# Modulation products of four channel blocks in four column groups, from the ninth block on

## The chip, the cores and the metric

The kernel runs on one core of one Trainium2 chip. The metric is the device time of one execution in microseconds (us). The kernel before takes 954.64 us, the median of three runs (954.42 to 954.87).

## The reference

One layer of a hybrid state-space and convolution block. `x` is 512 x 2048 and the context is 256 x 2048. What matters here is the first step:

```
def _adaln(cond, w_ada, b_ada):
    mod = jax.nn.silu(cond) @ w_ada + b_ada          # w_ada is 2048 x 6144
    return mod[..., :D_MODEL], mod[..., D_MODEL:2 * D_MODEL], mod[..., 2 * D_MODEL:]
def _modulate(v, shift, scale):
    return (_layernorm(v) * (1.0 + scale) + shift).astype(v.dtype)
...
    shift, scale, gate = _adaln(c, w_ada, b_ada)
    shift_c, scale_c, gate_c = _adaln(c_ctx, w_ada, b_ada)
    h = _modulate(x, shift[:, None], scale[:, None])
    hc = _modulate(ctx, shift_c, scale_c)
    u, z_s5, v, bg, cg, z_cv = _split_proj(h @ w_in)
    ...
        u_c = hc @ w_in[:, :D_S5]
```

Every one of the 2048 channels needs a shift and a scale for the latent rows and a shift and a scale for the context rows: a product of two vectors of 2048 with 2048 x 4096 weights, 32 MB in all. The rest of the layer (the state-space scan, the convolution, the gates, the output projection and the last LayerNorm) is not touched.

## The kernel before

**Blocks and tiles.** The channels stand in 16 blocks of 128. Block k's shift and scale weights arrive as two tiles of 1 MB, (k, 0) and (k, 1), one for each half of the 2048 inputs. They share a ring of seven buffers, `wa` (`RB = 7`), with the six 1 MB tiles of `x` and the context. `fill()` asks for the next tile in the order of the list `ring` as soon as the tile seven places earlier has been marked used; the request goes out on GpSimd's queue (POOL), and the instruction waits there until the matmuls that read the old contents of the buffer are done.

**Products.** `ada(k, hf)` runs eight matmuls for one tile: the stationary operand is a 128 x 32 slice of `cs` (the two condition vectors after SiLU, padded to 32 columns), the moving operand 256 columns of the tile. Matmul j writes partitions 32 * (j mod 4) on of the PSUM tile `aps`, so four matmuls in a row go to four column groups of TensorE, and four partial sums of block k stand below each other. `combine(k)` then copies `aps` to SBUF on ScalarE (`part`), transposes it in two TensorE instructions into `cps` (the other half of the same PSUM bank), and adds the four partial sums and the bias on VectorE into `ss`, 0.5 us in three instructions.

**The loop of the head.** `head()` holds all of this and the first quarter of the input projection. Its steady part is the loop over k from 3 to 15. One step does, in this order: `ada(k, 0)`, `ada(k, 1)`, the copy of `combine(k)`, a first `half()`, the transposition and sums of `combine(k)`, a second `half()`, and `mod(k)`. The two `half()` calls run the projection for block k - 2: nine 128 x 512 matmuls for the latent rows and twelve 128 x 256 ones for the context in the first, twelve more 128 x 256 ones in the second (`lat`, `cxt`, PSUM tiles `acc`). The third matmul of each group reads `wlo`, the low part of the projection weights, which VectorE splits off two items ahead. `mod(k)` makes the modulated channels: ScalarE writes `hi`, VectorE `xl`, `xc` and `lo`, for use two steps later. `some(us)` lets VectorE do a planned number of microseconds of the state-space parameters (`s5_params`) before and after the main part of `mod`. After k = 15 two more steps of `half()` finish the projection of blocks 14 and 15.

**Order.** The order of the instructions on every engine is the order in which this code is written; each engine works its own queue strictly in that order. A clock of planned costs (`_Clock`) decides where the background generators are called later in the kernel. `s5_params` waits for `room`, since it takes two `wa` buffers itself, and copies its powers (`PW`) on POOL, in the same queue as the `wa` requests.

Of the kernel before, what the change touches and what calls it, by code (L numbers as in the profile page):

```python
# [12 lines left out]
OP = mybir.AluOpType  # L13

P = 128
D = 2048
KT = 16
# [127 lines left out]
def tile_hybrid_s5_shortconv(  # L145
# [8 lines left out]
    ve, ac = _Timed(nc.vector, "dve", clk), _Timed(nc.scalar, "act", clk)  # L154
    pe, gp, sp = _Timed(nc.tensor, "pe", clk), _Timed(nc.gpsimd, "pool", clk), _Timed(nc.sync, "sp", clk)
# [30 lines left out]
    cs = base.tile([P, KT, 32], F32, name="cs")  # L186
    ss = base.tile([P, KT, 2, 2], F32, name="ss")
    bss = base.tile([P, KT, 2], F32, name="bss")
# [6 lines left out]
    def tt(out, a, b, op, e=None):  # L195
        (e or ve).tensor_tensor(out, a, b, op=op)
# [21 lines left out]
    def ahead(i):  # L218
        while st["load"] < min(i + LA + 1, len(items)) or st["split"] < min(i + SA + 1, len(items)):
            if st["split"] < min(i + SA + 1, st["load"]):  # L220
                j = st["split"]
                hi, lo = items[j][2]()
                r = raws.pop(j)
                ac.activation(hi, r, AF.Copy)
                tt(lo, r, hi.bitcast(F32), OP.subtract)
                his[j] = (hi, lo)
                st["split"] += 1
            else:
                load()
# [249 lines left out]
    def head():  # L479
        with pool(name="head", bufs=1) as hp, \  # L480
# [9 lines left out]
            ve.memset(epst, EPS)  # L490


            order = [(k, hf) for k in range(KT) for hf in range(2)]
            ring = [("x", q) for q in range(4)] + order[:2] + [("x", q) for q in (4, 5)] + order[2:]
            rows, used = {}, set()

            def fill(e=None):
                while len(rows) < len(ring):
                    n = len(rows)
                    if n >= RB and ring[n - RB] not in used:  # L500
                        return
                    t = rows[ring[n]] = hp.tile([P, D], F32, name="wa", tag="wa", bufs=RB)
                    a, b = ring[n]
                    if a != "x":
                        (e or gp).dma_start(t, wada_ss[a, b])
                    elif b == 0:
                        for f in range(4):
                            sp.dma_start(t[:, f * 512:(f + 1) * 512], x_in[0:P, f * 512:(f + 1) * 512])
                    else:
                        sp.dma_start(t, x_in[b * P:(b + 1) * P] if b < 4 else ctx_in[(b - 4) * P:(b - 3) * P])  # L510
# [4 lines left out]
            lam = hp.tile([P, 3, NG], F32, name="lam")  # L515
# [3 lines left out]
            aps = ps.tile([P, 512], F32, name="aps")  # L519
            aps, cps = aps[:, 0:256], aps[:, 256:512]  # L520
# [51 lines left out]
            def ada(k, hf):  # L572
                w = rows[k, hf].rearrange("p (k c) -> p k c", k=8)
                for j in range(8):
                    pe.matmul(aps[32 * (j % 4):32 * (j % 4) + 32], cs[:, hf * 8 + j], w[:, j],
                              start=hf == 0 and j < 4, stop=hf == 1 and j > 3)
                used.add((k, hf))
                fill()

            def lat(k, whi, wlo):  # L580
                lh, ll = hhi[k], hlo[k]
                for m in range(3):
                    wh, wl = whi[:, m * P:(m + 1) * P], wlo[:, m * P:(m + 1) * P]
                    for n_, (w, a) in enumerate(((wh, lh), (wh, ll), (wl, lh))):
                        pe.matmul(acc[m], w, a, start=k == 0 and n_ == 0, stop=k == KT - 1 and n_ == 2)

            def cxt(k, hf, whi, wlo):
                ch, cl = chi[k], clo[k]
                for j in range(4):
                    m = 4 * hf + j  # L590
                    wh, wl = whi[:, j * P:(j + 1) * P], wlo[:, j * P:(j + 1) * P]
                    ca = acc[3 + m // 2][:, (m % 2) * 256:(m % 2) * 256 + 256]
                    for n_, (w, b) in enumerate(((wh, ch), (wh, cl), (wl, ch))):
                        pe.matmul(ca, w, b, start=k == 0 and n_ == 0 and m % 2 == 0,
                                  stop=k == KT - 1 and n_ == 2 and m % 2 == 1, skip_group_check=True)

            def combine(k, e=None):
                part = hp.tile([P, 256], F32, name="part", tag="part")
                ac.activation(part, aps, AF.Copy)
                yield  # L600
                for f in range(2):
                    pe.transpose(cps[:, f * P:(f + 1) * P], part[:, f * P:(f + 1) * P], ident)
                s = ss[:, k]
                p4 = cps.rearrange("p (f j m) -> p f m j", f=2, j=4)[:, :, 0:2]
                ve.tensor_reduce(s, p4, op=OP.add, axis=mybir.AxisListType.X)
                tt(s, s, bss[:, k].unsqueeze(2).to_broadcast([P, 2, 2]), OP.add)
                ve.tensor_scalar(s[:, 1], s[:, 1], 1.0, None, op0=OP.add)
                yield

            def mod(k, parts, between=None):  # L610
                for x, hi, lo, new, m in parts:
                    hi[k], lo[k] = new("hi", F32R), new("lo", F32R)
                    ac.activation(hi[k], x[k], AF.Identity, scale=ss[:, k, 1, m:m + 1], bias=ss[:, k, 0, m:m + 1])
                if between:
                    between()
                for x, hi, lo, new, m in parts:
                    ve.tensor_scalar(x[k], x[k], ss[:, k, 1, m:m + 1], ss[:, k, 0, m:m + 1], op0=OP.mult, op1=OP.add)
                    tt(lo[k], x[k], hi[k].bitcast(F32), OP.subtract)

            lpart, cpart = (xl, hhi, hlo, slot, 0), (xc, chi, clo, cslot, 1)  # L620
# [7 lines left out]
            def split(n):  # L628
                while st["split"] < n:
# [7 lines left out]
                    if st["load"] < st["split"] + 5:  # L637
                        load()

            comb = {k: combine(k) for k in range(KT)}  # L640
            run(stats(0))
            run(norm(0))
# [16 lines left out]
            n4 = norm(4)  # L659
            mod(0, [lpart], lambda: [next(n4) for _ in range(5)])  # L660
            lat(0, *his[0])
            run(n4)
            next(comb[1])
# [15 lines left out]
            next(comb[3])  # L679
            mod(2, [lpart, cpart])  # L680
            st["pos"] = 2
            params = s5_params(hp, cps, lam, lambda: (13, 0) in used)

            def some(us):
                t0 = ck["dve"]
                while ck["dve"] < t0 + us:
                    try:
                        if next(params) == "stall":
                            return
                    except StopIteration:  # L690
                        return

            def half():
                i = st["pos"]
                ahead(i)
                k, hf = head_order[i]
                w = his.pop(i)
                if hf == 0:
                    lat(k, *w)
                cxt(k, hf, *w)  # L700
                st["pos"] += 1

            for k in range(3, KT):
                if k > 3:
                    ada(k, 0)
                    ada(k, 1)
                    next(comb[k])
                half()
                next(comb[k])
                half()  # L710
                mod(k, [lpart, cpart], lambda: some(1.0))
                some(1.0)
            while st["pos"] < 2 * KT:
                half()
                some(2.6)
# [181 lines left out]
    for k in range(13, KT):  # L897
        keep_item(k)

    head()  # L900


# [569 lines left out]
```

## Time and profile before

| | |
|---|---|
| median of 3 runs | 954.64 us |
| the profiled execution | 952.72 us |
| its span, first to last instruction | 950.7 us |
| TensorE busy in the span | 915.6 us, 96% |
| VectorE, ScalarE, GpSimd busy | 673.1, 379.2, 129.2 us |
| granted TensorE clock, mean | 0.994 |
| the loop step of k = 8, from its first product to the next step's | 84.82 to 92.06 us, 7.24 us |

Times in the rows are from the start of the span. In the rows, a TensorE product of `ada` is one instruction that the trace shows as two entries, so that 16 instructions read x32. The records of one name follow each other without a gap where a step's busy time is equal to its length.

### The profile page before, as it was taken

The page shows a single profiled execution, that of the slowest core. Times are in us where ns is not written, and L with a number is a line of the kernel's source. Part 1 is how long each engine was busy: PE and PEld are TensorE (multiplying, and loading weights), DVE is VectorE, ACT ScalarE, POOL GpSimd, SP SyncE. Part 2 cuts the span into 40 slices and gives each one's busy share as a digit, 9 for nine tenths or more (in the row PEclk, how much of TensorE's full clock was granted, in tenths as well). Part 3 has the DMA queues.
Part 4 walks back from the last instruction along what each step waited for, and adds up shares of the span by engine and source line. Part 5 has one row for each costly group of instructions (what it writes and reads, how often), then busy time and mean ns, then how long its engine had stood idle before and what let it go on. Part 6 is the DMA issues. An engine that isn't in the chain of part 4 may idle for free.

```text
span 950.7 us, 15381 instructions
## 1 busy us (share of the span) xinstructions
PE 915.6 (96%) x5488; PEld 746.7 (79%) x5488; DVE 673.1 (71%) x1553; ACT 379.2 (40%) x673; POOL 129.2 (14%) x267
## 2 busy tenths in 40 slices
PE   3899999999999999999999999999999999999994
PEld 3677887788888888888888888888888877787883
DVE  7779884478588889898767384642247789795577
ACT  4643343344343422224446444554444432224222
POOL 2211402111020000001222203020100023300000
PEclk9999999999999999999999999999999999999998
DMA  9999848987484233344565537363597578947322
GB/s 352 423 424 407 318 142 235 351 257 233 137 288 149 101 90 111 92 120 129 141 162 169 163 116 215 107 187 105 160 294 273 204 265 310 328 160 255 99 81 96
DMA packets 97100, 196.08 MB, mean 206 GB/s; under 512 B 26800, under 2 KB 33008, under 8 KB 92160
## 3 DMA queue, kind: packets, MB, share of 16 engines
q1 hardware_dynamic: 67216, 109.09, 35.5%
q0 software_dynamic: 18160, 78.80, 23.3%
q10 hardware_dynamic: 11648, 7.21, 2.4%
q8 instruction: 43, 0.70, 0.3%
q14 instruction: 33, 0.27, 0.1%
HBM read 177.37 MB, written 17.69 MB: 205 GB/s over the span
## 4 chain that ended last, share of the span: by engine, by line
PE 92%; DMA 3%; DVE 3%; ACT 1%; issue 1%; SPq 0%; ACTq 0%; POOL 0%; POOLq 0%
PE mm L139 65%; PE bg L139 15%; PE acc L139 9%; PE aps L139 3%; DMA Ud<-ut 2%; DMA wa<-in_wada_ss_dram 1%; DVE res L139 1%; DVE bst L139 1%; DMA wa<-in_x_dram 1%; ACT xc L139 0%; DVE wa L139 0%; DVE xc L139 0%; DVE sd L139 0%; SPq L139 0%; ACT hi L139 0%
## 5 line engine op out<-in xcount | busy, mean ns | idle before, releaser
L139 ACT ACTIVATE whi<-raw 128x512 fp32r<-128x512 f32 x276 | 171.6, 629 | 311.5 <-PE mm L139 204.8
L139 PE MATMUL mm<-hi,whi 128*128 128x512 f32 x720 | 283.7, 394 | 0.8 <-ACT whi L139 0.8
L139 DVE TENSOR_TENSOR wlo<-raw,whi 128x512 fp32r<-128x512 f32 x276 | 187.7, 688 | 133.7 <-ACT whi L139 125.0
L139 PE MATMUL mm<-lo,whi 128*128 128x512 f32 x720 | 280.6, 390 | 0.0
L139 PE MATMUL mm<-hi,wlo 128*128 128x512 f32 x720 | 280.6, 390 | 0.0
L139 PEld LDWEIGHTS mm<-hi,whi 128*128 128x128 f32 x720 | 135.1, 188 | 32.1 <-issue 2.4
L139 PEld LDWEIGHTS mm<-hi,wlo 128*128 128x128 f32 x720 | 135.1, 188 | 29.5 <-DVE wlo L139 0.9
L139 PEld LDWEIGHTS mm<-lo,whi 128*128 128x128 f32 x720 | 135.2, 188 | 26.9
L139 PE MATMUL acc<-hi,whi 128*128 128x256 f32 (+1 forms) x176 | 58.5, 332 | 0.0
L139 PE MATMUL acc<-lo,whi 128*128 128x256 f32 (+1 forms) x176 | 55.6, 316 | 0.0
L139 PE MATMUL acc<-hi,wlo 128*128 128x256 f32 (+1 forms) x176 | 55.2, 313 | 0.0
L139 POOL DMA_DIRECT2D gw<-in_wada_g_dram x64 | 34.3, 537 | 146.2 <-DVE gacc L139 112.4
L139 DVE SCALAR_TENSOR_TENSOR gacc<-gw,cs,gacc 128x512 f32<-128x512 f32 x60 | 44.9, 749 | 1.2
L139 PEld LDWEIGHTS acc<-hi,whi 128*128 128x128 f32 x176 | 33.5, 190 | 8.9 <-issue 6.6
L139 ACT ACTIVATE hxx<-vst 64x512 f32<-64x512 f32 x32 | 36.1, 1128 | 2.6 <-DVE ks L139 2.3
L139 PEld LDWEIGHTS acc<-hi,wlo 128*128 128x128 f32 x176 | 33.6, 191 | 2.3
L139 PEld LDWEIGHTS acc<-lo,whi 128*128 128x128 f32 x176 | 33.7, 191 | 2.0
L139 PE MATMUL aps<-wa,cs 128*32 128x256 f32 x512 | 31.7, 387 | 3.4 <-DVE ss L139 2.5
L139 PE MATMUL acc<-ident,wa 128*128 128x128 f32 x96 | 15.8, 332 | 16.3 <-DVE wa L139 15.7
L139 DVE TENSOR_TENSOR sc<-MT,vst 128x128 f32<-128x128 f32 x128 | 30.9, 281 | 0.0
L139 ACT ACTIVATE cvv<-mm 128x512 f32<-128x512 f32 x24 | 14.3, 596 | 39.7 <-PE mm L139 39.7
L139 PEld LDWEIGHTS acc<-ident,wa 128*128 128x128 f32 x96 | 14.0, 174 | 18.0 <-DVE wa L139 15.5
(216 smaller groups left out, 1523.2 us busy)
## 6 DMA issues: line engine op xcount, KB each, us to landing
raw<-in_w_m_dram SPq DMA_DIRECT2D x180, 256.0 KB, 2.9
wa<-in_wada_ss_dram POOLq DMA_DIRECT2D x30, 1024.0 KB, 10.0
gw<-in_wada_g_dram POOLq DMA_DIRECT2D x64, 256.0 KB, 5.4
raw<-in_w_out_dram SPq DMA_DIRECT2D x64, 256.0 KB, 4.1
raw<-in_w_u_dram SPq DMA_DIRECT2D x32, 256.0 KB, 8.0
btt<-in_bt_dram POOLq DMA_DIRECT2D x16, 512.0 KB, 6.6
pwt<-Wd POOLq DMA_DIRECT2D x16, 512.0 KB, 5.5
uu<-Ud POOLq DMA_DIRECT2D x16, 384.0 KB, 6.1
```

The costliest lines, as they stand in the source:

```text
L139: return f(*a, **k)
```

## The change

For blocks 0 to 7 nothing changes. From block 8 on, four blocks are treated together (8 to 11 and 12 to 15). `ada4(g, hf)` runs 32 matmuls: column group i belongs to block g + i, and the loop goes over j outside and over the four blocks inside, so every group sums all of its 16 products in PSUM and no partial sums are left. `ada4(g, 0)` stands at the end of the step of k = g - 1, `ada4(g, 1)` at the beginning of the step of k = g. One copy, one transposition (two instructions) and two VectorE instructions then serve four blocks; the steps of k = 9, 10, 11, 13, 14 and 15 have no products and no transposition. The ring asks for the four first halves and then the four second halves of a group. VectorE's share of parameter work moves: 0.8 planned us in place of 1.0, twice a step, in the steps of k = 9, 10, 13, 14 and 15, and 2.0 in those of k = 7 and 11; and `room` opens with tile (12, 0) in place of (13, 0).

```
-            order = [(k, hf) for k in range(KT) for hf in range(2)]
+            order = [(k, hf) for k in range(8) for hf in range(2)]
+            order += [(k, hf) for g in (8, 12) for hf in range(2) for k in range(g, g + 4)]
...
+            def ada4(g, hf):
+                w = [rows[k, hf].rearrange("p (k c) -> p k c", k=8) for k in range(g, g + 4)]
+                for j in range(8):
+                    for i in range(4):
+                        pe.matmul(aps[32 * i:32 * i + 32], cs[:, hf * 8 + j], w[i][:, j],
+                                  start=hf == 0 and j == 0, stop=hf == 1 and j == 7)
+                used.update((k, hf) for k in range(g, g + 4))
+                fill()
...
+                if k > 7:
+                    s = ss[:, k:k + 4]
+                    p4 = cps.rearrange("p (f i m) -> p i f m", f=2, i=4)[:, :, :, 0:2]
+                    tt(s, p4, bss[:, k:k + 4].unsqueeze(3).to_broadcast([P, 4, 2, 2]), OP.add)
+                    ve.tensor_scalar(s[:, :, 1], s[:, :, 1], 1.0, None, op0=OP.add)
+                    yield
+                    return
...
-            params = s5_params(hp, cps, lam, lambda: (13, 0) in used)
+            params = s5_params(hp, cps, lam, lambda: (12, 0) in used)
...
-                if k > 3:
+                us = 1.0
+                if 3 < k < 8:
                     ada(k, 0)
                     ada(k, 1)
+                elif k in (8, 12):
+                    ada4(k, 1)
+                if k < 9 or k == 12:
+                    if k > 3:
+                        next(comb[k])
+                    half()
                     next(comb[k])
+                else:
+                    us = 0.8
+                    half()
                 half()
-                next(comb[k])
-                half()
-                mod(k, [lpart, cpart], lambda: some(1.0))
-                some(1.0)
+                if k in (7, 11):
+                    ada4(k + 1, 0)
+                    us = 2.0
+                mod(k, [lpart, cpart], lambda: some(us))
+                some(us)
```

TensorE's queue where the step of k = 7 ends and that of k = 8 begins (`acc` are the projection's sums, `aps` the products), as a difference:

```order
 L139 MATMUL acc_181<-lo,whi 128x256
 L139 MATMUL acc_181<-hi,wlo 128x256
-L139 MATMUL aps<-wa,cs 32x256 x16
+L139 MATMUL aps<-wa,cs 32x256 x64
 L139 MATMUL acc_175<-hi,whi 128x512
 L139 MATMUL acc_175<-lo,whi 128x512
 L139 MATMUL acc_175<-hi,wlo 128x512
```

The products of eight tiles now stand in one string, with nothing else between them; the same is to be seen for k = 12.

Inside that string, with tile numbers and waits: before, `wa_803` is (8, 0) and `wa_896` is (8, 1).

```order
L139 MATMUL aps_182<-wa_803,cs_111 32x256 [waits DMASW4_49,DVE_49]
L139 MATMUL aps_182<-wa_803,cs_111 32x256 x7
L139 MATMUL aps_182<-wa_896,cs_111 32x256 [waits DMASW5_49]
L139 MATMUL aps_182<-wa_896,cs_111 32x256 x7
```

Now `wa_803` is (8, 0), 896, 906 and 993 are (9, 0) to (11, 0), and 1003, 1096, 1106 and 1192 are (8, 1) to (11, 1); the last row of `ada4(8, 0)` is the fourth here.

```order
L139 MATMUL aps_182<-wa_803,cs_111 32x256
L139 MATMUL aps_182<-wa_896,cs_111 32x256
L139 MATMUL aps_182<-wa_906,cs_111 32x256
L139 MATMUL aps_182<-wa_993,cs_111 32x256
L139 MATMUL aps_182<-wa_1003,cs_111 32x256 [waits DMASW0_49]
L139 MATMUL aps_182<-wa_1096,cs_111 32x256 [waits DMASW1_49]
L139 MATMUL aps_182<-wa_1106,cs_111 32x256 [waits DMASW2_49]
L139 MATMUL aps_182<-wa_1192,cs_111 32x256 [waits DMASW3_49]
```

The fourth product of `ada4(8, 1)` reads the tile that is seven requests behind `wa_803`, four instructions after the last read of `wa_803`.

POOL's queue, from the request of (8, 0) on, as it stands now:

```order
L139 DMA wa_803<-in_wada_ss_dram 128x2048 [waits DMASW5_49,PE_49]
L139 DMA wa_896<-in_wada_ss_dram 128x2048 [waits DMASW6_49,PE_49]
L139 DMA wa_906<-in_wada_ss_dram 128x2048 [waits DMASW7_49,PE_49]
L139 DMA wa_993<-in_wada_ss_dram 128x2048 [waits DMASW0_49,PE_49]
L139 DMA wa_1003<-in_wada_ss_dram 128x2048 [waits DMASW1_49,PE_49]
L139 DMA wa_1096<-in_wada_ss_dram 128x2048 [waits DMASW2_49,PE_49]
L139 DMA wa_1106<-in_wada_ss_dram 128x2048 [waits DMASW3_49,PE_49]
L139 DMA wa_1192<-in_wada_ss_dram 128x2048 [waits DMASW4_49,PE_49]
```

The eighth row takes the buffer of the first, so its wait for TensorE (PE) is for the last read of `wa_803`. Further on, the last request of the ring, (15, 1), now stands behind all of the `PW` copies of POOL, where before three pairs of them stood between the last three requests.

## Rows read from the trace of the kernel before

**Rows 1.** The page's head, its busy times, and one group of part 5.
```profile
span 950.7 us, 15381 instructions
...
PE 915.6 (96%) x5488; PEld 746.7 (79%) x5488; DVE 673.1 (71%) x1553; ACT 379.2 (40%) x673; POOL 129.2 (14%) x267
...
L139 PE MATMUL mm<-hi,whi 128*128 128x512 f32 x720 | 283.7, 394 | 0.8 <-ACT whi L139 0.8
```

**Rows 2.** Busy time by stretch: length, PE, PEld, DVE, ACT, POOL, PEclk, DMA, GB/s.
```profile
84.82:92.06 7.24, 7.24 (x69) 5.77 (x68) 6.68 (x26) 3.27 (x6) 1.17 (x2) 1.00 1.00 395
...
142.74:150.00 7.26, 5.69 (x37) 4.60 (x36) 2.68 (x5) 3.14 (x8) 3.38 (x4) 1.00 0.37 108
```

**Rows 3.** The chain of waits, 84.8 to 160 us: start, length, what.
```profile
84.89 1.86 PE aps L139 x32
86.75 3.73 PE acc L139 x21
90.48 0.22 PE aps L139 x2
90.70 1.43 PE acc L139 x12
...
145.91 9.89 PE acc L139 x66
```

**Rows 4.** Timeline of POOL, 71 to 88 us: start, length, instruction, idle before.
```profile
79.84 0.53 POOL L139 DMA_DIRECT2D wa<-in_wada_ss_dram  x1 [0.34 <-PE aps L139]
86.22 0.64 POOL L139 DMA_DIRECT2D wa<-in_wada_ss_dram  x1 [5.85 <-PE aps L139]
```

**Rows 5.** DMA issues of five short stretches (79.8, 86.2, 93.4, 94.3, 111.6): us to landing.
```profile
wa<-in_wada_ss_dram POOLq DMA_DIRECT2D x1, 1024.0 KB, 9.5
...
wa<-in_wada_ss_dram POOLq DMA_DIRECT2D x1, 1024.0 KB, 6.5
...
wa<-in_wada_ss_dram POOLq DMA_DIRECT2D x1, 1024.0 KB, 8.0
...
wa<-in_wada_ss_dram POOLq DMA_DIRECT2D x1, 1024.0 KB, 10.1
...
wa<-in_wada_ss_dram POOLq DMA_DIRECT2D x1, 1024.0 KB, 5.1
```

**Rows 6.** Timeline of PE, 31.5 to 39 us.
```profile
32.01 1.07 PE L139 MATMUL aps<-wa,cs 128*32 128x256 f32 x16 [1.91 <-DVE ss L139]
33.91 1.59 PE L139 MATMUL aps<-wa,cs 128*32 128x256 f32 x16 [0.83 <-DMA wa<-in_wada_ss_dram]
...
36.45 0.63 PE L139 MATMUL acc<-hi,wlo 128*128 128x512 f32 x1
...
38.42 0.39 PE L139 MATMUL acc<-hi,wlo 128*128 128x512 f32 x1
```

**Rows 7.** Busy time by stretch, 34 to 38 us.
```profile
34.00:38.00 4.00, 4.00 (x23) 2.48 (x24) 3.50 (x9) 0.90 (x2) 0.53 (x1) 0.57 1.00 410
```

**Rows 8.** Timeline of DVE, 84.82 to 92.06 us.
```profile
86.20 0.54 DVE L139 TENSOR_SCALAR xl<-xl,ss 128x512 f32<-128x512 f32 x1
...
88.17 0.65 DVE L139 TENSOR_SCALAR pt<-pt 128x64 f32<-128x64 f32 x3
...
89.11 0.23 DVE L139 TENSOR_TENSOR pt<-pt,pt 128x64 f32<-128x64 f32 x1
...
90.73 0.17 DVE L139 TENSOR_REDUCE ss<-aps 128x4 f32<-128x16 f32 x1
...
91.22 0.69 DVE L139 TENSOR_TENSOR wlo<-raw,whi 128x512 fp32r<-128x512 f32 x1
91.83 0.29 DVE L139 TENSOR_SCALAR pt<-pt 128x64 f32<-128x64 f32 x2
```

**Rows 9.** Timeline of POOL, 104 to 118 us.
```profile
114.57 2.13 POOL L139 COPY PW<-pw 64x128 f32<-64x128 f32 x4 [0.73 <-DVE pw L139]
```

**Rows 10.** Timeline of PE, 142.5 to 146 us.
```profile
143.65 0.44 PE L139 MATMUL aps<-ident,PI 128*128 128x128 f32 x2 [0.62 <-ACT WT L139]
```

## The prediction

> **What bounds the kernel now.** I read the page first: TensorE is busy for 96% of the span, and behind the head its products wait for nothing but one 0.8 us gap [rows 1]. So a microsecond that TensorE gains or loses in the head moves the end by a microsecond; there is no later slack that gives it back. Then the busy time by stretch, one stretch for each step of the head's loop: in the step of k = 8 TensorE works for all of its 7.24 us, VectorE for 6.68 us, and the 16 DMA engines are at a share of 1.00 with 395 GB/s [rows 2]. The reader is to see that TensorE sets the pace, with VectorE close behind. The chain of waits divides the step: products 1.86, first half 3.73, transposition 0.22, second half 1.43 us; it repeats so from k = 4 to k = 15 [rows 3]. The two steps at the end of the head that have neither products nor a transposition take 9.89 us together, so 5.0 each [rows 3]. Products, transposition and the changes between these kinds of matmul therefore cost 7.24 - 5.0 = 2.24 us a step.
>
> **What the change takes away on TensorE.** Before, four blocks cost 4 x 2.24 = 9.0 us for this. Now they cost four strings of the old 16 instructions, 4 x 1.86 = 7.44 us, since the same 64 matmuls on four column groups remain, and one transposition of 0.22: 7.66 us. That saves 1.3 us for four blocks and 2.6 us for eight. The sure part is six transpositions, 6 x 0.22 = 1.3 us; the other 1.3 us is what the changes between kinds of matmul cost. I take 2.6, with 1.3 as the other end. ScalarE loses six copies and VectorE a few tenths a step; neither is the bound, so I count them only below, in VectorE's account.
>
> **What it adds: two waits for a load.** The string of `ada4(8, 0)` and `ada4(8, 1)` reads eight tiles, and the ring has seven buffers. The eighth, (11, 1), goes into the buffer of (8, 0), which `ada4(8, 0)` reads until its last four instructions. The order shows the first read of (11, 1) four instructions behind that, with nothing in between. So TensorE must sit through one whole load from request to landing, and it does so again for (15, 1).
>
> How long: before, the string of k = 8 starts at 84.82 [rows 2], its first tile is done after half of 1.86 us, and POOL makes the next request at 86.22 [rows 4], so 1.40 - 0.93 = 0.47 us from the last read to the request. From request to landing the five single loads near this place took 5.1 to 10.1 us [rows 5]. The 5.1 belongs to a request with no other in front of it; 6.5 to one (86.22) behind one that was still under way; 8.0 and 10.1 to a pair in one go. The tile in question is the first of four requests that become free together, and the loads in front of it, (9, 1) and (10, 1), go out at the old times, the later at 79.84, landing 9.5 us later at 89.3 [rows 4, 5]. The new request goes out at 84.82 + 2 x 1.86 + 0.47 = 89.0, nearly free of it. First wait: 0.47 + 5.1 to 6.5 = 5.6 to 7.0 us; I take 6.0. For (15, 1) the load queue has been empty for some time, so I take the lower end, 5.6 us, and 7.0 as the other. The three followers stand behind (11, 1) in the same queue; if they shared the engines with it, the price would be nearer the 8.0 to 10.1 us rows, which is a rival below. What is queued behind the waiting product on TensorE is everything: the rest of the string, the copy that ScalarE makes of it, and with it the next split of ScalarE.
>
> POOL makes the request of (15, 1) behind the `PW` copies, which need VectorE. Four of them take 2.13 us [rows 9]. By the account of VectorE below, counted from the transposition of k = 8, the last power is ready after 7.8 + 5.2 + 6.2 = 19.2 us, and `ada4(12, 0)` ends after 1.43 + 5.0 + 0.9 + 5.0 + 0.8 + 5.0 + 3.7 = 21.8 us. That leaves room for the last two copies (1.07 us); I take nothing for it, and at most 1.5 us if VectorE is later.
>
> **The clock after each wait.** In the head there is one place where TensorE paused and went on: gaps of 1.91 and 0.83 us, with 1.07 us of products between them. Behind them 128x512 matmuls took 0.63 us in place of 0.39 [rows 6], and the granted clock was 0.57 on average from 34 to 38 us, that is mostly the lower level of 1.2 GHz [rows 7]. The loss there is 4 x (1 - 0.57) = 1.7 us. A wait of 5.6 us is longer than either gap, so I charge 1.7 us for each, 3.4 in all; the ends are 0 and 2.5 us each (5 us at half the clock, if it takes as long to rise as the wait lasted). The Trainium skill (TensorE: Matmul & The Clock Gate, HAM oscillation) warns of just this: a kernel whose products wait for a load in every round runs the next round at the low clock. By that rule the charge falls due twice; without it the sum would be 3.4 us lower, and rows 6 and 7 bear it out.
>
> **VectorE behind TensorE.** The steps without products are 5.0 us long, but VectorE's work in them is not shorter. From its rows [rows 8]: main part of `mod` 88.17 - 86.20 = 1.97; a split 91.83 - 91.22 = 0.61; the three scale sums 0.49, now two, 0.35; a 64-wide parameter operation 0.22 to 0.26. Take the end of the transposition of k = 8 as zero. VectorE then has the sums (0.35), a split (0.6), nine small operations (2.3), `mod` (1.97), six operations more with a few wide ones (1.9) and the split whose result TensorE needs in the step of k = 10 (0.6): 7.8 us. TensorE is at the third matmul of that step, the first that reads it, after 1.43 + 5.0 + 0.5 = 6.9 us. It waits 0.9 us. The next step has two splits, `mod` and some 2.7 us of wider parameter operations, 5.9 us against 5.0, for another 0.8 or so; the string of k = 12 and its load wait then let VectorE catch up. The same sum for k = 12 to 14 gives 0.7. Together 2.4 us, an estimate from those rows; the ends are 0 (operations that overlap more) and 4. It is cut off if the two load waits let VectorE work ahead, but VectorE's own queue has the scale sums in it, which wait for the transposition behind the load.
>
> **What stays.** The pauses while the state-space tables are transposed (0.62 us and two like it) [rows 10] stand one step earlier and are as long. The order of every engine behind the head is unchanged, so the rest of the kernel costs what it did.
>
> **Sum.** -2.6 + 6.0 + 5.6 + 3.4 + 2.4 = 14.8 us. The profiled execution took 952.72 us, its span of 950.7 and 2.0 around it [rows 1]; it would come to 967.5. The median of the runs is 1.9 us above that execution, so I add the 14.8 to the median: 954.64 + 14.8 = 969.4 us.
>
> **Rivals.** First, *only the two loads*. The clock stays up or falls inside the wait, and VectorE keeps up. For it: two of the last terms are estimates, and the 0.62 us pauses [rows 10] did not lower the clock (1.00 in the stretch that has them [rows 2]). Against it: these pauses are a tenth as long as a load. -2.6 + 5.6 + 5.6 = 8.6 us, 963.2. Second, *long loads*. The four requests that come free together divide the engines. For it: the pair of 93.4 and 94.3 took 8.0 and 10.1 us [rows 5]. Against it: the second of the pair, asked for 0.9 us later, took 2.1 us longer, so it landed 3.0 us behind the first: they went one behind the other. With 8 to 10 us for both waits (plus 0.47) the sum is -2.6 + 2 x 9.5 + 3.4 + 2.4 = 22.2 us, 976.8. Third, on the other side, *the eighth tile is there in time*. If its request went out 5.1 us before TensorE comes to the string's fourth product of the second half, so before 83.4, both waits and what hangs on them would be gone, and the saving of 2.6 us remain: 952.0. For it: before, requests ran a ring ahead, and loads of up to 10.1 us [rows 5] delayed no product of the loop. Against it: the buffer is read until 88.5, and the order has the load wait for that. It decides only if a request can be made before the old contents are read, which the order denies. Fourth, that the change does nothing that can be measured: a wait of 2.6 us in all that cancels the saving would need loads of a quarter of the shortest row.
>
> **How the numbers follow.** The forecast, loads with clock and VectorE (10 to 19 us), 0.70; only the loads 0.13; long loads 0.11; in time 0.03; no change 0.03. The lower end of the range is 962, where the saving is 2.6 and both waits are 5.0, a little under the shortest row; the upper end 976, which has 7.0 for both waits, 2.5 each for the clock, 4 for VectorE and 1.3 saved (20.7 us, 975.3), and a little of the long loads. Faster by over 0.2% (1.9 us, about what these runs can tell from no change): 0.03, the third rival. Within 0.2%: 0.03. Slower: 0.94.
>
> **What would show it.** In the profile of the changed kernel TensorE should be idle for 5 to 7 us twice, at about 88 to 95 us and some 33 us later, with a load of `wa` as what ended it, three products into the second half of each string. The loads of (11, 1) and (15, 1) should be the only ones that TensorE waits for in the loop. The granted clock should be at its lower level for some microseconds behind each. In the steps of k = 10, 11 and 14 short waits for `wlo` should stand; if they don't, the 2.4 us are wrong. Steps without products should take 5.0 us where nothing waits. If TensorE shows no gap in the strings, the whole forecast is wrong; if the gaps are 8 us or longer, the second rival is right.

## The result and the profile after

The changed kernel takes 969.7 us, the median of six runs (967.36 to 972.72), against 954.53 us for the kernel before (six runs beside it); the ratio is 1.0175, 95% interval 1.0161 to 1.0189. By the medians it is 15.2 us slower, by the ratio 16.7; 969.4 us was forecast, 14.8 us slower.

The profiled execution is the slowest of the six, 972.72 us with a span of 970.7, so it lies 20.0 us over the profiled one of before, not 15. Head and busy times of its page, and three groups of part 5; below them the last of these groups as it was before:

```profile
span 970.7 us, 15324 instructions
...
PE 919.9 (95%) x5476; PEld 747.6 (77%) x5476; DVE 670.7 (69%) x1533; ACT 376.3 (39%) x667; POOL 130.0 (13%) x267
...
L139 PE MATMUL mm<-hi,whi 128*128 128x512 f32 x720 | 283.9, 394 | 1.9 <-ACT whi L139 1.9
...
L139 PE MATMUL acc<-hi,wlo 128*128 128x256 f32 (+1 forms) x176 | 56.2, 320 | 1.1 <-DVE wlo L139 1.1
...
L139 PE MATMUL aps<-wa,cs 128*32 128x256 f32 x512 | 36.5, 429 | 16.1 <-DMA wa<-in_wada_ss_dram 13.8
```

```profile
L139 PE MATMUL aps<-wa,cs 128*32 128x256 f32 x512 | 31.7, 387 | 3.4 <-DVE ss L139 2.5
```

TensorE has twelve instructions less than before [rows 1] and is busy for 4.3 us more: the products that took 387 ns each now take 429. In front of them it now waits 16.1 us, where it waited 3.4; 13.8 of the 16.1 are for a load of `wa`, 11.6 of these in the two strings. The 0.8 us gap behind the head has become 1.9.

The timeline of TensorE around the two strings (start, length, instruction, idle before and what ended it):

```profile
85.79 4.29 PE L139 MATMUL aps<-wa,cs 128*32 128x256 f32 x70
94.86 6.21 PE L139 MATMUL aps<-wa,cs 128*32 128x256 f32 x58 [4.78 <-DMA wa<-in_wada_ss_dram]
...
133.50 5.67 PE L139 MATMUL aps<-wa,cs 128*32 128x256 f32 x58 [6.80 <-DMA wa<-in_wada_ss_dram]
```

Each string of 128 entries stops after 70, that is after 64 entries of its first half and six of the three products that read (8, 1) to (10, 1) or (12, 1) to (14, 1), and goes on when the eighth tile has landed. The first fence has the requests of the two late tiles in POOL's timeline: the first of the three at 89.73, and 126.56. The second has the time from request to landing of each (its last number, us):

```profile
89.73 1.56 POOL L139 DMA_DIRECT2D wa<-in_wada_ss_dram  x3 [8.39 <-PE aps L139]
91.60 0.53 POOL L139 DMA_DIRECT2D wa<-in_wada_ss_dram  x1 [0.31 <-issue]
...
123.02 0.95 POOL L139 COPY PW<-pw 64x128 f32<-64x128 f32 x2 [1.42 <-DVE pw L139]
126.56 0.53 POOL L139 DMA_DIRECT2D wa<-in_wada_ss_dram  x1 [2.59 <-PE aps L139]
```

```profile
wa<-in_wada_ss_dram POOLq DMA_DIRECT2D x1, 1024.0 KB, 5.1
...
wa<-in_wada_ss_dram POOLq DMA_DIRECT2D x1, 1024.0 KB, 6.9
```

Both requests wait for the products (`<-PE aps`), as the order had it; before, such a request stood a ring ahead of its use [rows 4]. The `PW` copies are done 2.6 us before the second request, so they delay nothing.

Now the loop as a whole, from the first matmul of step 7 to the first one behind the head, and the three stretches in it in which the clock was low (length, PE, PEld, DVE, ACT, POOL, PEclk, DMA, GB/s). First before, then after:

```profile
79.44:155.64 76.20, 74.63 (x650) 60.99 (x647) 61.07 (x198) 29.95 (x54) 16.03 (x31) 1.00 0.71 262
```

```profile
94.86:100.10 5.24, 5.24 (x52) 2.50 (x56) 0.00 (x0) 0.00 (x0) 0.00 (x0) 0.50 1.02 428
133.50:137.65 4.15, 4.15 (x40) 1.97 (x44) 0.00 (x0) 0.00 (x0) 0.00 (x0) 0.50 0.00 0
158.13:161.54 3.41, 3.41 (x11) 2.62 (x10) 0.69 (x1) 0.72 (x2) 2.91 (x4) 0.50 0.41 115
80.41:174.15 93.74, 79.61 (x638) 62.69 (x635) 58.72 (x178) 27.02 (x48) 16.41 (x31) 0.91 0.58 214
```

The loop grew by 93.74 - 76.20 = 17.5 us. TensorE's pauses in it are 93.74 - 79.61 = 14.1 us against 1.6: +12.6. Its granted clock is 0.50, the 1.2 GHz level, for 5.24 + 4.15 us behind the two waits and 3.41 us behind the table transpositions; half of the 12.8 us is lost: +6.4. What is left of its busy time is 79.61 - 6.4 = 73.2 against 74.63: -1.4. This is not the whole saving, since TensorE's slow restarts behind its waits count as busy; the run without the eighth tile below sizes both. The other 2.5 of the 20.0 us lie outside of the loop: 0.97 ahead of it (79.44 to 80.41) and 1.5 behind it, 1.1 of them the longer gap behind the head.

Why the profiled execution is slower than most: of the six, two have a mean granted clock of 0.987 and spans of 965.4 and 966.0 us, the others 0.982 to 0.984 and 967.6 to 970.7. If TensorE had work in all of that time, the 0.005 between them is 0.005 x 970 = 4.9 us lost. That fits a low clock that lasts longer in some executions than in others; only one of the six has a trace, so where it lay in the others is not shown.

### The profile page after: what moved, and what is told of

Same layout as the page of the kernel before. It is cut to its first block, busy times and chain, and to the rows that moved or that the text cites. A ratio compares the mean times of both kernels' runs of the same rounds, so it can differ in the third digit from the quotient of the medians.

```text
span 970.7 us, 15324 instructions
## 1 busy us (share of the span) xinstructions
PE 919.9 (95%) x5476; PEld 747.6 (77%) x5476; DVE 670.7 (69%) x1533; ACT 376.3 (39%) x667; POOL 130.0 (13%) x267
## 4 chain that ended last, share of the span: by engine, by line
PE 83%; issue 6%; DMA 6%; DVE 3%; POOL 1%; ACT 1%; SPq 0%; ACTq 0%; POOLq 0%; DVEq 0%
PE mm L139 62%; PE bg L139 15%; PE acc L139 4%; DMA wa<-in_wada_ss_dram 2%; DMA Ud<-ut 2%; PE aps L139 2%; DMA graw<-Gd 1%; POOL wa L139 1%; DVE res L139 1%; DVE bst L139 1%; DMA wa<-in_x_dram 1%; DVE wlo L139 0%; DVE PI L139 0%; DVE wa L139 0%; DVE sd L139 0%
## 5 line engine op out<-in xcount | busy, mean ns | idle before, releaser
L139 PE MATMUL aps<-wa,cs 128*32 128x256 f32 x512 | 36.5, 429 | 16.1 <-DMA wa<-in_wada_ss_dram 13.8
L139 PEld LDWEIGHTS aps<-wa,cs 128*32 128x32 f32 x512 | 17.4, 122 | 31.5 <-DMA wa<-in_wada_ss_dram 15.2
L139 PE MATMUL acc<-ident,wa 128*128 128x128 f32 x96 | 14.8, 317 | 17.2 <-DVE wa L139 17.2
```

The source lines that it names most:

```text
L139: return f(*a, **k)
```

## The experiments

The theory is *load wait*: each group costs TensorE one load from request to landing, since the string of eight tiles runs in a ring of seven, then some microseconds of low clock, and VectorE's lag a little. Rivals are *plan* (the new division of VectorE's work costs the time) and *string* (the joined strings are slower by themselves). "Over" is the ratio to the kernel before, run beside it, less one, times 953.5 us; by this measure the change is 16.7 us over.

**One group only.** Blocks 8 to 11 as before, 12 to 15 together.

```
-            order = [(k, hf) for k in range(8) for hf in range(2)]
-            order += [(k, hf) for g in (8, 12) for hf in range(2) for k in range(g, g + 4)]
+            order = [(k, hf) for k in range(12) for hf in range(2)]
+            order += [(k, hf) for g in (12,) for hf in range(2) for k in range(g, g + 4)]
...
-                if 3 < k < 8:
+                if 3 < k < 12:
...
```

> Only blocks 12 to 15 are treated together; blocks 8 to 11 keep their own products. Theory 'load wait' (each group costs one wait of TensorE for the load of its eighth tile, then the low clock): -1.3 us saved, one wait of 6.8 us, 2.1 us of low clock, 0.3 us for VectorE, so about 8 us over the kernel before (6 to 11), half of the change's 15. TensorE idle 6 to 7 us once, in the string of k = 12. Rival 'plan' (the new plan of VectorE's parameter work costs the time): that plan is changed from k = 11 on only, so 2 to 5 us, with no gap in the string. Rival 'string' (joined strings of products run slower by themselves): half of 15, but with the string's matmuls themselves slower and no gap.

Measured: 965.38 us, ratio 1.0115 (1.0096 to 1.0133), 11 us over, the upper end of what was expected. TensorE's timeline in the string, and its longest wait behind the head:

```profile
119.59 0.93 PE L139 MATMUL aps<-wa,cs 128*32 128x256 f32 x2 [3.53 <-DMA wa<-in_wada_ss_dram]
122.51 5.64 PE L139 MATMUL aps<-wa,cs 128*32 128x256 f32 x58 [1.99 <-DMA wa<-in_wada_ss_dram]
...
713.10 0.50 PE L139 MATMUL mm<-hi,whi 128*128 128x512 f32 x1 [2.81 <-ACT whi L139]
```

The gap is 5.5 us, in two parts, since (14, 1) also comes late here; one of 6 to 7 us was expected. The loop is 84.58 us long in its profile, 8.4 over before, as the theory has it. The profiled span is 12.7 us over, though: the loop starts 1.8 us earlier, and 6.1 us more lie behind the head. Waits for split weights there, 1.19, 0.28 and 2.81 us against one of 0.82 before, make 3.5 of these, and behind the longest the granted clock is 0.57 from 713.1 to 717.0 us. So the 11 us are not the group's wait alone. *Plan* gave 2 to 5 us and no gap, so as the main cause it falls here.

**VectorE's plan alone.** The kernel before, with the new planned times.

```
-                mod(k, [lpart, cpart], lambda: some(1.0))
-                some(1.0)
+                us = 2.0 if k in (7, 11) else 0.8 if k in (9, 10, 13, 14, 15) else 1.0
+                mod(k, [lpart, cpart], lambda: some(us))
+                some(us)
```

> The kernel before with the new plan for VectorE alone (2.0 planned us at k = 7 and 11; 0.8 at 9, 10, 13, 14 and 15), products as before. 'Load wait': within 2 us of the kernel before, since TensorE has no wait in the loop. 'Plan': at least half of the 15 us, 7 us or more over the kernel before. 'String': 0.

Measured: 954.26 us, ratio 1.0020 (1.0005 to 1.0035), 1.9 us over. Its timeline shows where: the heavy part of k = 7 makes the next products wait for the scale sums.

```profile
91.67 1.93 PE L139 MATMUL aps<-wa,cs 128*32 128x256 f32 x32 [1.40 <-DVE ss L139]
121.04 1.93 PE L139 MATMUL aps<-wa,cs 128*32 128x256 f32 x32 [0.38 <-DVE ss L139]
```

*Plan* as the main cause falls: 1.9 of 16.7 us, and in the change itself that wait does not come up; its string at 85.79 has no idle time in front of it.

**TensorE kept at work during the load.** Products of a zero tile, with a resident operand, are added to the same sums between the halves of a string.

```
...
+                if hf == 0:
+                    for _ in range(9 if g == 8 else 14):
+                        for i in range(4):
+                            pe.matmul(aps[32 * i:32 * i + 32], zero, xc[15], start=False, stop=False)
...
```

> The changed kernel with 36 and 56 matmuls of zeros (32x256, on all four column groups, added to the same sums) between the two halves of the strings of k = 8 and k = 12: TensorE works while the load comes, about 3.9 and 6.0 us of the waits of 4.8 and 6.8. 'Load wait' with the clock as a cost of its own: the granted clock stays at its upper level in both strings and the time falls by 4 to 6 us against the changed kernel, to 9 to 11 us over the kernel before. If the clock is no cost of its own (the waits alone explain it): as the changed kernel, 14 to 16 us over.

Measured: 966.39 us, ratio 1.0132 (1.0114 to 1.0150), 12.6 us over, so 4.1 us less than the change (1.0175). That is the lower end of the fall that was expected; 9 to 11 us over was missed by 1.6. The interval does not touch that of the change (1.0161 to 1.0189), so the fall is clear of noise. The stretches of the same places, behind the loads, and the two strings:

```profile
94.80:100.00 5.20, 5.20 (x66) 3.29 (x60) 0.68 (x1) 0.91 (x2) 1.83 (x4) 1.00 1.03 422
129.80:135.00 5.20, 5.20 (x68) 3.24 (x66) 0.52 (x1) 0.90 (x2) 0.00 (x0) 1.00 0.01 3
```

```profile
94.65 3.64 PE L139 MATMUL aps<-wa,cs 128*32 128x256 f32 x58 [2.19 <-DMA wa<-in_wada_ss_dram]
...
123.26 6.23 PE L139 MATMUL aps<-xc,zero 128*32 128x256 f32 x112
129.30 4.20 PE L139 MATMUL aps<-wa,cs 128*32 128x256 f32 x64
```

With the clock at 1.00 what is left of the first string takes 3.64 us where it took 6.21. Its load is still awaited (6.5 us to landing here, 5.1 in the change), and the filler ended 2.19 us too early. In the second string the filler covers the load (6.1 us, 6.9 in the change), and no gap is left. From its first product to the first matmul behind it, the first string takes 14.04 us against 15.21 in the change and the second 13.66 against 16.49, so 4.0 us less together. The two loads were 0.6 us longer together, so the gain does not come from them: it is the clock, a cost of its own of about 4 us for the two waits.

**The halves apart.** The same products with projection work between the two halves of a group.

```
-                elif k in (8, 12):
-                    ada4(k, 1)
...
                 half()
+                if k in (8, 12):
+                    ada4(k, 1)
+                    next(comb[k])
+                    half()
+                    next(comb[k])
+                else:
+                    if k < 8:
+                        next(comb[k])
+                    if k == 7:
+                        ada4(8, 0)
+                    half()
+                    if k == 10:
+                        ada4(12, 0)
...
```

> The same products, copies and transpositions as in the change, but the two halves of a group stand apart: the first half of the products for 8 to 11 behind the transposition of k = 7, the second behind the first half of step 8 (5.2 us of projection between them); for 12 to 15 the first half stands at the end of step 10 and the second behind the first half of step 12 (8.7 us between them). 'Load wait': the load has time to land, both waits and the low clock go, and what is left is the saving less some waits for VectorE: 3 us faster to 2 us slower than the kernel before, most likely 1 us faster. 'Plan' and 'string': still 10 us or more over the kernel before, since VectorE's plan and the number of products are those of the change.

Measured: 956.22 us, ratio 1.0031 (1.0019 to 1.0043), 3.0 us over. Five sixths of the loss are gone with the same products and the same plan for VectorE, so *plan* falls as the main cause. *String* is not decided here, since the strings are no longer joined; the next run does that. The 3.0 us are 1 us more than the upper end that *load wait* gave. What is left, from its timeline:

```profile
83.17 3.66 PE L139 MATMUL aps<-wa,cs 128*32 128x256 f32 x64 [0.68 <-DVE ss L139]
93.13 3.64 PE L139 MATMUL aps<-wa,cs 128*32 128x256 f32 x58 [0.61 <-DMA wa<-in_wada_ss_dram]
105.22 0.50 PE L139 MATMUL acc<-hi,wlo 128*128 128x512 f32 x1 [1.21 <-DVE wlo L139]
119.89 0.50 PE L139 MATMUL acc<-hi,wlo 128*128 128x512 f32 x1 [0.69 <-DVE wlo L139]
135.10 0.50 PE L139 MATMUL acc<-hi,wlo 128*128 128x512 f32 x1 [1.06 <-DVE wlo L139]
```

The waits for `wlo` are the lag of VectorE that was forecast, 3.0 us here; in the change it is 1.1.

**Without the eighth tile.** Everything stands where the change put it, but (11, 1) and (15, 1) are not loaded.

```
-            order += [(k, hf) for g in (8, 12) for hf in range(2) for k in range(g, g + 4)]
+            order += [(k, hf) for g in (8, 12) for hf in range(2) for k in range(g, g + 4 - hf)]
...
-                w = [rows[k, hf].rearrange("p (k c) -> p k c", k=8) for k in range(g, g + 4)]
+                w = [rows[min(k, g + 3 - hf), hf].rearrange("p (k c) -> p k c", k=8) for k in range(g, g + 4)]
```

> The changed kernel without the eighth tile of each group: (11, 1) and (15, 1) are neither loaded nor read, the products of the second half of blocks 11 and 15 read the tiles of blocks 10 and 14 instead (so two of the 32 loads and the right modulation of these two blocks are left out). Every instruction of TensorE, VectorE and ScalarE stands where the change put it. 'Load wait': both gaps and the low clock behind them go, and the time falls by 11 to 16 us against the changed kernel, to 0 to 4 us over the kernel before. Rival 'plan' (VectorE's order costs the most) or 'string' (the joined strings cost the most): no more than 3 us less than the changed kernel.

Measured: 955.39 us, ratio 1.0017 (1.0004 to 1.0031), 1.6 us over and some 15 us less than the change. Its loop:

```profile
79.29:155.00 75.71, 72.65 (x638) 59.87 (x634) 58.64 (x178) 27.03 (x48) 15.36 (x29) 1.00 0.64 243
```

One load a group carries nearly the whole loss, with the order of all other work unchanged; this is the plainest test of the theory, and *plan* and *string* both fall by it as main causes. TensorE is busy for 72.65 us against 74.63, so 2.0 us less, and its pauses are 3.1 us against 1.6.

The 2.0 us are not the saving, though. The timeline shows the saving where nothing waits, and what a wait costs beyond its gap:

```profile
98.11 0.40 PE L139 MATMUL acc<-hi,whi 128*128 128x512 f32 x1
...
103.05 0.40 PE L139 MATMUL acc<-hi,whi 128*128 128x512 f32 x1
...
104.13 0.50 PE L139 MATMUL acc<-hi,wlo 128*128 128x512 f32 x1 [0.46 <-DVE wlo L139]
...
108.73 0.40 PE L139 MATMUL acc<-hi,whi 128*128 128x512 f32 x1
...
114.45 7.11 PE L139 MATMUL aps<-wa,cs 128*32 128x256 f32 x128
121.50 0.50 PE L139 MATMUL acc<-hi,whi 128*128 128x512 f32 x1
...
126.79 0.40 PE L139 MATMUL acc<-hi,whi 128*128 128x512 f32 x1
```

An unbroken string of 64 products takes 7.05 us (114.45 to 121.50), against 4 x 1.86 = 7.44 for the four strings before, so a joined string is not slower by itself. The rest of its step, with the transposition, takes 5.29 us (121.50 to 126.79), and a step without products 4.94 (98.11 to 103.05). A group comes to 7.05 + 5.29 + 3 x 4.94 = 27.2 us, where four steps took 4 x 7.24 = 29.0: 1.8 us saved, some 3.5 us for both groups. But the step with a gap of 0.46 us is 5.68 us long (103.05 to 108.73), 0.74 more than 4.94. Likewise a wait of 0.50 us for a load makes the first string 8.16 us long, 1.11 more than 7.05. What a wait costs beyond its gap counts as busy time, and so the busy time hides part of the saving.

The loop is 0.5 us shorter than before (75.71 against 76.20). The profiled execution is the lowest of twelve; where the 1.6 us of the medians lie is not shown.

**Apart, with less work for VectorE.** The edit is against the kernel with the halves apart.

```
-                us = 1.0 if k < 9 or k == 12 else 0.8
+                us = {7: 1.5, 8: 0.5, 9: 0.6, 10: 0.6, 11: 2.0, 12: 0.5, 13: 0.6}.get(k, 1.0)
...
-                if k in (7, 11):
-                    us = 2.0
```

> As the kernel with the two halves of a group apart, which was 3.0 us over the kernel before and still had 3 us of waits for split weights, but with less parameter work of VectorE in the steps without products (planned 1.5 at k = 7; 0.5, 0.6, 0.6 at 8 to 10; 2.0 at 11; 0.5, 0.6 at 12 and 13; 1.0 at 14 and 15). If VectorE's lag is what is left of the price: the waits for split weights fall under 0.5 us together and the time by 2.5 to 4 us, to 0.5 us over to 1.5 us under the kernel before. If the saving of 2.6 us on TensorE isn't there: 1 to 2 us over, without such waits.

Measured: 956.86 us, ratio 1.0037 (1.0022 to 1.0053): nothing gained. The waits of steps 10 and 12 fall to 0.15 us and less, but the parameter work now ends one step later and new ones stand at the end of the loop:

```profile
136.90 0.50 PE L139 MATMUL acc<-hi,wlo 128*128 128x512 f32 x1 [0.36 <-DVE wlo L139]
143.49 0.50 PE L139 MATMUL acc<-hi,wlo 128*128 128x512 f32 x1 [1.35 <-DVE wlo L139]
```

The expectation failed. VectorE's work was moved, not lessened, and it came late in other steps of 5 us.

**Six buffers.** `RB = 6` in the kernel before and in the changed one.

> The kernel before with six ring buffers in place of seven. Its loads land 3 us or more ahead of their use in the loop, so no wait comes up there; the start of the head may shift by 1 to 3 us. 0 to 3 us over the kernel before; the measure for the next kernel.

> The changed kernel with six ring buffers: two tiles of each group, (10, 1) and (11, 1), and (14, 1) and (15, 1), now wait for buffers of the group's own first half. 'Load wait': each gap grows by the time in which one more 1 MB load follows the first, 2.4 to 3 us, so 5 to 6 us, and by 0 to 2 us of low clock: 5 to 8 us more than the changed kernel after what six buffers cost the kernel before is taken off. 'Plan' and 'string': no more than the kernel before loses by it.

Measured: before with six, 954.71 us, ratio 1.0010 (0.9997 to 1.0023), not to be told from no change. The change with six, 977.6 us, ratio 1.0254 (1.0232 to 1.0276), so 1.0254 / 1.0010 over 1.0175, 6.6 us more than the change with seven. Its waits:

```profile
97.54 1.06 PE L139 MATMUL aps<-wa,cs 128*32 128x256 f32 x2 [4.71 <-DMA wa<-in_wada_ss_dram]
100.33 5.26 PE L139 MATMUL aps<-wa,cs 128*32 128x256 f32 x58 [1.73 <-DMA wa<-in_wada_ss_dram]
...
136.47 1.06 PE L139 MATMUL aps<-wa,cs 128*32 128x256 f32 x2 [5.26 <-DMA wa<-in_wada_ss_dram]
138.91 6.44 PE L139 MATMUL aps<-wa,cs 128*32 128x256 f32 x58 [1.38 <-DMA wa<-in_wada_ss_dram]
```

A second late tile a group makes a second wait, as the theory says, and the time is in its range. But the profiled gaps, 6.4 and 6.6 us, are not 2.4 to 3 us longer than the 4.8 and 6.8 of the change: TensorE does products between the two loads, and the first load of the second string took 5.4 us here and 6.9 there. Between the two profiles the loop grows by only 2.0 us (95.74 against 93.74), and it starts 2.6 us later, as it starts 2.0 later in the kernel before with six. So these profiles do not show the reason that was given for the range; how the 6.6 us of the medians divide is not settled by these two profiles.

## Why the prediction was right

The mechanism was read off the order, and the runs without the eighth tile (1.0017) and with the halves apart (1.0031) bear it out. The single terms, in us, in the profiled execution, with TensorE's time as busy time and gaps:

| step | forecast | measured | from |
|---|---|---|---|
| saving on TensorE, less slow restarts | -2.6 | -1.4; -2.0 without the eighth tile | busy time of the loop |
| first load wait | 6.0 | 4.8 | timeline, string of k = 8 |
| second load wait | 5.6 | 6.8 | timeline, string of k = 12 |
| low clock behind them | 3.4 | 4.7 | stretches at 0.50 |
| VectorE behind TensorE | 2.4 | 1.1 | gaps before `wlo` |
| sum | 14.8 | 16.0 | |
| low clock at the table transpositions | 0 | 1.7 | stretch at 0.50 |
| outside of the loop | 0 | 2.5 | 0.97 ahead, 1.5 behind |

(The pauses of the table transpositions fell by 0.2 us.) The last two rows belong to this execution more than to the change: neither with the filler nor without the eighth tile is the clock low at the transpositions, and the median of the runs is 3 us below the profiled one. So the hit to 0.3 us owes something to errors of both signs. It also owes something to the base: by the ratio the change costs 16.7 us, 1.9 more than forecast.

One sum of the prediction is wrong. The terms given for the upper end, 14.0 + 5.0 + 4.0 - 1.3, make 21.7 us and 976.3, not 20.7 and 975.3, so they reach just past the 976 of the range. In VectorE's account the first sum is 7.7, not 7.8, which takes 0.1 us off the 2.4.

- *The saving* was put too small: 2.6 us were to leave TensorE's work, and where nothing waits some 3.5 do. The term that was short is the strings: four had been kept at their old 7.44 us, and joined they take 7.05. What a step loses with its transposition, 7.24 - 1.86 - 4.94 = 0.44 us, was in the forecast at about this size. The busy time shows less because of the restarts behind waits.
- *The first wait* was put too long because I let the load take up to 6.5 us, with the two loads in front of it still under way. They were done: the later, asked for at 80.81, took 8.6 us, to 0.3 us ahead of the request at 89.73. The load took 5.1, as short as the shortest of [rows 5]. And where I had counted 0.47 us from the last read to the request as waiting, the request went out 0.35 us before TensorE ran out of products (89.73 against 85.79 + 4.29), since behind the last read of that buffer it still had three products of the first half and three of the second to do.
- *The second wait* was put too short: I took the lone load at the lowest row, and it took 6.9 us; the request again went out ahead, by 0.14 us.
- *The clock.* One row of a low stretch behind gaps of 1.91 and 0.83 us [rows 6, 7] carried the term. The filler shows it to be a cost by itself, 4.1 us by the ratios. The 5.24 and 4.15 us at half clock lose 2.6 and 2.1 us, where 1.7 each was charged; the first is just above the upper end of 2.5. The Trainium skill (TensorE: Matmul & The Clock Gate, HAM oscillation) names the mechanism, products that wait for a load and then run at the low clock, and these stretches agree with it.
- *VectorE* waits fell in the steps that were named, k = 10, 11 and 14, with gaps of 0.46, 0.41 and 0.26 us, half of the 2.4 in all. In the change the steps of k = 10 and 11 are 5.69 and 5.72 us long, though, against 4.93 for k = 9, so with the restarts the term is an estimated 2 us. The account of its queue was right in place, and a little too high in size.
- *The rivals.* Only the two loads (963.2, a ratio of 1.009) and no change: excluded, the interval begins at 1.0161. Long loads: the first of the four requests was not slowed by the three behind it (5.1 us). The eighth tile in time: excluded by the two gaps.

No version here beats the kernel before. Without the eighth tile, about 2 of the 3.5 us saved go into waits for VectorE and 1.1 into the short wait for a load in the first string. With the halves apart the gaps before `wlo` alone are 3.0 us. Without any wait the edit could give those 3.5 us, under 0.4%.

## What to carry to other kernels

Before work is batched over more tiles, count the tiles that one unbroken string on an engine reads and compare them with the ring: one more than it has buffers means nearly a whole load, from request to landing, in the middle of the string, however far ahead the loads ran before. Price such a wait with the low clock behind it; here that added some 40% to the gaps. Size a saving from the start of one stretch to the start of the next where nothing waits; here the busy time hid more than a third of it. And look at which engine is second in the steps that the batching shortens, since its work does not get shorter with them.

## What was not expected

A 1 MB load with no other in front of it took from 4.9 to 6.9 us from request to landing: 5.1 and 6.9 in the change, 4.9 with the halves apart. The 6.9 was the one with the emptiest queue, asked for at 126.56 and landed at about 133.5; from 131 us on the engines moved 90 and 25 GB/s, as the following stretches of the change show. So a few late packets seem to have set the landing; why they were late was not tried.

```profile
130.00:131.00 1.00, 0.00 (x0) 0.00 (x0) 0.93 (x5) 0.00 (x0) 0.00 (x0) 0.91 0.88 336
131.00:132.00 1.00, 0.00 (x0) 0.00 (x0) 0.93 (x6) 0.00 (x0) 0.00 (x0) 0.50 0.23 90
132.00:133.00 1.00, 0.00 (x0) 0.00 (x0) 0.37 (x2) 0.00 (x0) 0.00 (x0) 0.50 0.06 25
```

The three short pauses at the table transpositions, 0.47 us each with transpositions of 0.44 us between them, were followed by 3.41 us at the 1.2 GHz level in the profile of the change, and by none in that of before, where they were 0.62, 0.47 and 0.47 us [rows 10]. With VectorE's plan alone they were 0.62, 0.47 and 0.47 us too, and there the clock did fall: the third transposition took 0.69 us, and the granted clock was 0.58 from 146.2 to 149.4. So pauses of one length are followed by a low clock in one execution and by none in another; what decides it is not shown.

```profile
145.47 0.69 PE L139 MATMUL aps<-ident,PI 128*128 128x128 f32 x2 [0.47 <-ACT WT L139]
```
